# A mixture of experts in which three of eight experts get 64 slots instead of 128

## The chip, the cores and the metric

The kernel runs on one core of one Trainium2 chip. The metric is the time of one execution in microseconds of the device; the median of three runs stands for a kernel. The matrices are float32. TensorE is called PE, VectorE DVE, ScalarE ACT, GpSimd POOL and SyncE SP, as in the profile.

## The reference, cut to what matters

Two transformer blocks of two layers each are applied to 256 tokens of width 1024. The last feed-forward part is a mixture of eight experts, of which each token uses two:

```python
logits = (t @ router)                       # 256 tokens, 8 experts
top_v, top_i = lax.top_k(logits, 2)
top_w = softmax(top_v)
gate = sum(one_hot(top_i, 8) * top_w[..., None], axis=1)
y = 0
for e in range(8):                          # wg, wu: 1024 x 3584, wd: 3584 x 1024
    y = y + gate[:, e:e+1] * ((silu(t @ wg[e]) * (t @ wu[e])) @ wd[e])
```

The result of a layer norm over `ALPHA * x + y` is the output. The 512 pairs of token and expert come to 64 for an expert on average.

## The kernel before

Every product of float32 matrices is made of three fast matmuls (`mm3`): each operand is split into a high part, rounded to the fast type, and a low part, the rest; high x high, low x high and high x low are added up in PSUM. Weights come from memory in units of 1 MB on SP's queue into `raw` buffers (`Weights.load`). ACT makes the high part of a piece of 1024 columns a partition (`Weights.high`), DVE, or at times POOL, the low part (`Weights.low`), into one of five piece buffers, up to three pieces ahead of PE (`LOOK = 3`). When the low part of a unit's last piece is made, its `raw` buffer is free and SP may start the next transfer.

The order of the instructions on each engine is written out when the kernel is built. A planner (`Ctx`, `Meter`) keeps a clock for each engine with estimated costs; work beside the main chain of PE is a generator that is stepped when the clock of PE passes the moment at which its input is ready (`Ctx.tick`). In `Weights.low` the planner puts a low part on POOL if POOL's clock would end it over 1000 ns before DVE's:

```python
dve = max(m.t["vector"], m.floor) + 1.04 * n
eng = g.nc.gpsimd if g.calm or pool() + POOL < dve and not g.quiet else g.nc.vector
```

The expert stage is the end of the kernel. `begin` computes the router, and the first chunk (512 of the 3584 columns) of expert 0 for all 256 tokens. `route` finds each token's two experts, its place in the expert's list (`m.pos`), the counts and the gates. `gather` builds a 0/1 matrix (`pm`) from the places and copies the tokens of one expert with it into 128 slots, split into high and low (`xg`). `expert` goes through seven chunks of 512 columns: 16 gate products and up products (`up`, each three matmuls with a stationary 128 x 128 block of tokens and 512 moving columns of weights), Silu on ACT, the product on DVE, four transposes on PE, the split into high and low by ACT and DVE (`fT`), and eight `down` products into two banks that are kept through the expert. `finish` brings the 128 slots back to the 256 tokens with the transposed 0/1 matrix and adds them, times the gate, to the sums (`ys`). The experts go in the order 0 to 7. Eleven `raw` buffers of 1 MB feed them (two more at the start), made from memory that the other stages no longer need.

PSUM has eight banks. After the loop the largest count is read into registers; if it is over 128, a second pass over all experts handles the slots from 128 on, otherwise a branch skips it.

Of the kernel before, what the change touches and what calls it, by code (L numbers as in the profile page):

```python
# [17 lines left out]
P = 128  # L18
# [53 lines left out]
def tables3():  # L72
    j = np.arange(P)[:, None]
    t = np.arange(P)[None, :]
    up = np.where(j < t, 1.0, 0.0)
    slot = np.broadcast_to(np.arange(S)[None, :], (P, S))
    return np.ascontiguousarray(np.concatenate([up, np.ones((P, P)), slot], 1).astype(np.float32))
# [102 lines left out]
class Weights:  # L180
# [10 lines left out]
    def add(self, src, a, b, cuts):  # L191

        u = len(self.units)
        self.units.append((src, a, b))
        for i, c in enumerate(cuts):
            self.cuts.append((u, c, i == len(cuts) - 1))

    def load(self, upto=None):
        g = self.g
        m = g.m  # L200
        while self.loaded < min(upto or len(self.units), len(self.units)) and g.free["raw"]:
            src, a, b = self.units[self.loaded]
            buf = g.take("raw")
            raw = buf[:, :a * b].rearrange("p (a b) -> p a b", a=a)
            c = 0
            for s in src if isinstance(src, list) else [src]:
                n = s.shape[-1]
                g.tc.nc.sync.dma_start(raw[:, :, c:c + n], s.rearrange("(k p) n -> p k n", p=P))
                c += n
            m.t["sync"] = max(m.t["sync"], m.ready[g.key(buf)]) + 1.45 * a * b  # L210
            m.ready[g.key(buf)] = m.t["sync"] + 2000
            self.raw[self.loaded] = (buf, raw)
            self.loaded += 1

    def ahead(self, upto):
# [3 lines left out]
        while self.split <= min(upto, len(self.cuts) - 1) and g.free["piece"]:  # L219
            u, (k0, k1, c0, c1), last = self.cuts[self.split]  # L220
            if u >= self.loaded:
                self.load(u + 1)
            buf, raw = self.raw[u]
# [1692 lines left out]
E, FF = 8, 3584  # L1916
NC = FF // 512
# [10 lines left out]
def plan_expert(g, ws, li, e, begun=False):  # L1928
    a = g.a

    def up(c):
        for name in ("moe_w_gate_2", "moe_w_up_2"):
            for k0 in (0, 4):
                ws.add(a[name][li, e][k0 * P:(k0 + 4) * P, c * 512:(c + 1) * 512], 4, 512, [(0, 2, 0, 512), (2, 4, 0, 512)])

    def down(c):
        if e == E - 1 and c == NC - 1:
            for k in range(4):
                r0 = c * 512 + k * P
                ws.add(a["moe_w_down_2"][li, e][r0:r0 + P, :], 1, D, [(0, 1, 0, 512), (0, 1, 512, D)])  # L1940
            return
        for k0 in (0, 2):
            r0 = c * 512 + k0 * P
            ws.add(a["moe_w_down_2"][li, e][r0:r0 + 2 * P, :], 2, D, [(0, 1, 0, D), (1, 2, 0, D)])
# [4 lines left out]
class Moe:  # L1949


    def __init__(self, g):
# [4 lines left out]
        c3 = big[:, 4096:4608]  # L1957
        g.nc.sync.dma_start(c3, g.a["cst3"])
        self.before, self.ones, self.slot = c3[:, 0:P], c3[:, P:2 * P], c3[:, 2 * P:512]
        self.fT = [g.mid([P, 2, 4, P], F32R)]  # L1960
        self.ys = [big[:, 4608:5632], g.mid([P, D])]
# [26 lines left out]
    def last_vectors(self):  # L1988

        g = self.g  # L1990
        wb = g.big("b", [P, 2, D])
# [14 lines left out]
    def lend_slots(self):  # L2006
# [3 lines left out]
        self.slots = [g.big(s, [P, 2048]) for s in "ab"]  # L2010
# [3 lines left out]

    def after_mixer(self):
        self.lend(self.huge("b"), 3)

    def after_first(self):
# [4 lines left out]
        self.fT.append(f[:, 1024:2048].rearrange("p (a k n) -> p a k n", a=2, k=4))  # L2023


def route(g, m, po):
# [4 lines left out]
    yield lambda: len(g.free["small"]) >= 8 and g.free["t10"]  # L2031
# [7 lines left out]
    sm = [g.take("small") for _ in range(7)]  # L2039
# [3 lines left out]
    gate, pos = keep[:, 0:16], keep[:, 16:32]  # L2043
# [23 lines left out]
    m.pos, m.gate = pos, gate  # L2067
# [5 lines left out]
    m.done.mark("routed")  # L2073
    yield m.done.got("begun")

    for t in range(2):
# [9 lines left out]
        nc.vector.scalar_tensor_tensor(gate[:, e8], o1, g1, gate[:, e8], op0=ALU.mult, op1=ALU.add)  # L2086
        yield
    g.give(*sm[:6])


def begin(g, m, x, hT, ready):
# [7 lines left out]
    def at(t):  # L2099
        if t:  # L2100
# [3 lines left out]
            first.append(gather(g, m, x, 0, 0))  # L2104
# [13 lines left out]
    ft_ = m.fT[0]  # L2118
    ft = {"t": ft_, "done": False}

    def steps():
# [14 lines left out]
        ft["done"] = True  # L2136
    g.do(steps())

    def sums():
        yield lambda: ft["done"]  # L2140
# [8 lines left out]
def gather(g, m, x, e, s0):  # L2149
# [3 lines left out]

    xg_ = g.big("cab"[m.xg % 3] if not m.wb else "ca"[m.xg % 2], [P, 2, KD, P], F32R)
    m.xg += 1
    xg = [xg_[:, i] for i in range(2)]
    got = {"pm": None, "xg": xg, "n": 0}

    def steps():
        yield m.done.got("routed")  # L2160
# [4 lines left out]
        for t in range(2):  # L2165
            nc.vector.tensor_scalar(pm[:, t, :], m.slot[:, s0:s0 + P], m.pos[:, 8 * t + e:8 * t + e + 1], None,
                                    op0=ALU.is_equal)
        for q in range(2):
            yield "bank"
            p_ = g.take("bank")  # L2170
            for i in range(4):
                k = 4 * q + i
                for t in range(2):
                    nc.tensor.matmul(p_[:, i * P:(i + 1) * P], x[t][:, k * P:(k + 1) * P], pm[:, t, :],
                                     start=t == 0, stop=t == 1)
            yield
            pv = p_.rearrange("p (a b) -> p a b", a=4)
            nc.scalar.activation(xg[0][:, 4 * q:4 * q + 4], pv, AF.Copy)
            yield
            nc.vector.tensor_tensor(xg[1][:, 4 * q:4 * q + 4], pv, xg[0][:, 4 * q:4 * q + 4], op=ALU.subtract)  # L2180
            g.give(p_)
            got["n"] += 1
# [4 lines left out]
def expert(g, m, e, got, begun=None, following=None):  # L2187
# [7 lines left out]
    mine = m.count  # L2195

    def up(c):
        gu = []
        f = g.take("t20")
        for i in range(2):  # L2200
            o = g.take("bank")
            k = 0
            while k < KD:
# [3 lines left out]
                for j in range(2):  # L2207
                    mm3(g, o, xg[0][:, k, :], xg[1][:, k, :], hi[:, j, :], lo[:, j, :], k == 0, k == KD - 1)
                    k += 1
                    if j == 1:  # L2210
                        g.give(pc)
                    g.tick()
            gu.append(o)
            if i == 0:
                def sl(o=o):
                    g.act(f, o, AF.Silu)
                    g.give(o)
                g.do(sl)
        ft_ = m.fT[c % 2]
        ft = {"t": ft_, "done": False}  # L2220

        def steps():
            o = gu[1]
            nc.vector.tensor_tensor(f, o, f, op=ALU.mult)
            yield
            for i in range(4):
                nc.tensor.transpose(o[:, i * P:(i + 1) * P], f[:, i * P:(i + 1) * P], g.ident)
            g.give(f)
            yield
            pv = o.rearrange("p (a b) -> p a b", a=4)  # L2230
            nc.scalar.activation(ft_[:, 0], pv, AF.Copy)
            yield
            nc.vector.tensor_tensor(ft_[:, 1], pv, ft_[:, 0], op=ALU.subtract)
            g.give(o)
            ft["done"] = True
        g.do(steps())
        return ft

    def down(c, f):
        if not y:  # L2240
            y.extend(g.take("bank") for _ in range(2))
        g.until(lambda: f["done"])
        ft = f["t"]
        halves = e == E - 1 and c == NC - 1
        for k in range(4):
            for n in range(2):
                if n == 0 or halves:
                    hi, lo, pc = g.piece()
                s = slice(0, 512) if halves else slice(n * 512, (n + 1) * 512)
                mm3(g, y[n], ft[:, 0, k, :], ft[:, 1, k, :], hi[:, 0, s], lo[:, 0, s],  # L2250
                    c == 0 and k == 0, c == NC - 1 and k == 3)
                if n == 1 or halves:
# [17 lines left out]
    for kind, c in steps(begun):  # L2270
# [10 lines left out]
        if c == 2 and m.count == 1:  # L2281
            g.retire(*m.slots)
        if c == 3 and m.count == E - 1:
            g.do(m.last_vectors())

    def finish():
        yield m.done.got("pmT", mine)
        yield m.done.got("sums")
        yh = m.yh
# [4 lines left out]
        for t in range(2):  # L2294
            for n in range(2):
                yield "bank"
                o = g.take("bank")
                for i in range(2):
                    mm(o, m.pmT[:, tok(t)], yh[:, i, n, :], start=i == 0, stop=i == 1)
                yo = m.ys[t][:, n * 512:(n + 1) * 512]  # L2300
                gc = m.gate[:, 8 * t + e:8 * t + e + 1]
# [8 lines left out]
def experts(g, m, x, s0, got, begun=None):  # L2310
    for e in range(E):
        follow = (lambda e=e: gather(g, m, x, e + 1, s0)) if e < E - 1 else None
        got = expert(g, m, e, got, begun if e == 0 else None, follow)
# [39 lines left out]
def two_blocks(g, out):  # L2353
# [6 lines left out]
    for e in range(E):  # L2360
        plan_expert(g, g.w, 0, e, e == 0)
# [49 lines left out]
    for l in range(2):  # L2411
        mT, ready_k, over = second_mixer(g, x, l, hT, ready)
        moe = []
        after = [lambda: None, lambda: moe.append(Moe(g))][l]
# [4 lines left out]
    m, = moe  # L2419
    got, begun = begin(g, m, x, hT, ready)  # L2420
    g.early = EARLY_MOE
    experts(g, m, x, 0, got, begun)
    wb, = m.wb

    many = nc.values_load(m.cnt[0:1, 0:1], min_val=0, max_val=S)
    with g.tc.If(many > P):
        g.w = Weights(g)
        for e in range(E):
            plan_expert(g, g.w, 0, e)
        g.table = None  # L2430
        got = gather(g, m, x, 0, P)
        g.do(got["steps"])
        experts(g, m, x, P, got)
# [33 lines left out]
```

## Time and profile before

| | |
|---|---|
| median of 3 runs | 2414.9 us (2413.13 to 2416.1) |
| the profiled execution | 2413.49 us, span 2411.6 us |
| PE busy | 2357.7 us, 98% of the span |
| DVE busy | 1853.1 us, 77% |
| ACT busy | 1480.9 us, 61% |
| POOL busy | 373.6 us, 15% |
| granted clock of TensorE, mean | 0.993 |
| bytes moved | 577.70 MB, mean 240 GB/s |

The shares are averages over stages with different limits. Matmuls overlap in the record, so a busy PE may still have room; how matmuls follow one another tells more. Idle time counts on the engine that sets the pace.

### The profile page before, as it was taken

How to read it: one execution, taken by the hardware profiler on the slowest of the kernel's cores; microseconds unless marked ns; L12 is line 12 of the kernel's file. 1: busy time of each engine (PE TensorE's matmuls, PEld its weight loads, DVE VectorE, ACT ScalarE, POOL GpSimd, SP SyncE). 2: the span in 40 equal slices, each digit the busy share in tenths (PEclk: the TensorE clock that was granted, in tenths of full speed). 3: DMA queues.
4: the chain of work that ended last, by engine and by line, in shares of the span. 5: the costliest groups of instructions: out<-in, count | busy, mean ns of one | idle time of the engine just before them, and what ended most of it. 6: DMA issues, size and time to landing. Idle time of an engine off the chain costs nothing. (4 is left out here: it accounts for less than half of the span.)

```text
span 2411.6 us, 36624 instructions
## 1 busy us (share of the span) xinstructions
PE 2357.7 (98%) x13971; PEld 2039.8 (85%) x13971; DVE 1853.1 (77%) x2611; ACT 1480.9 (61%) x2126; POOL 373.6 (15%) x407
## 2 busy tenths in 40 slices
PE   8999999999999999999999899999999999999997
PEld 7799999988999988789878678888888888888785
DVE  6666987665589748765477788989898888898887
ACT  5664565465546646444446377777777777777674
POOL 4202433323043302210041300000000000000000
PEclk9999999999999999999999999999999999999998
DMA  7345555543555554455644789999999999999892
GB/s 242 123 144 189 162 190 189 179 135 128 175 175 170 190 191 155 151 158 192 209 131 141 265 310 327 349 347 346 349 359 359 332 357 350 352 346 355 316 354 93
DMA packets 317100, 577.70 MB, mean 240 GB/s; under 512 B 12818, under 2 KB 138354, under 8 KB 316660
## 3 DMA queue, kind: packets, MB, share of 16 engines
q1 hardware_dynamic: 316916, 575.28, 68.6%
q8 instruction: 111, 1.82, 0.3%
q14 instruction: 73, 0.60, 0.1%
HBM read 574.19 MB, written 1.05 MB: 239 GB/s over the span
## 5 line engine op out<-in xcount | busy, mean ns | idle before, releaser
L147 DVE TENSOR_TENSOR wlo<-raw,whi 128x1024 fp32r<-128x1024 f32 (+1 forms) x596 | 748.4, 1278 | 210.8 <-ACT whi L147 208.7
L147 ACT ACTIVATE whi<-raw 128x1024 fp32r<-128x1024 f32 (+1 forms) x628 | 637.9, 1042 | 153.1 <-PE bank L147 126.8
L147 PE MATMUL bank<-hTh,whi 128*128 128x256 f32 x1064 | 304.7, 286 | 0.2 <-ACT const L147 0.2
L147 PE MATMUL bank<-hTl,whi 128*128 128x256 f32 x1064 | 300.0, 282 | 0.0
L147 PE MATMUL bank<-hTh,wlo 128*128 128x256 f32 x1064 | 299.8, 282 | 0.0
L147 PE MATMUL bank<-whi,hTl 128*128 128x512 f32 (+2 forms) x732 | 255.3, 391 | 0.0
L147 DVE TENSOR_TENSOR wlo<-b24b,whi 128x1024 fp32r<-128x1024 f32 (+1 forms) x179 | 209.6, 1216 | 22.8 <-ACT whi L147 22.6
L147 PE MATMUL bank<-whi,b8a 128*128 128x512 f32 x672 | 212.2, 397 | 0.0
L147 PEld LDWEIGHTS bank<-hTh,whi 128*128 128x128 f32 x1064 | 200.6, 189 | 3.6 <-issue 1.5
L147 PE MATMUL bank<-whi,b8c 128*128 128x512 f32 x640 | 201.8, 396 | 0.0
L147 PEld LDWEIGHTS bank<-hTh,wlo 128*128 128x128 f32 x1064 | 200.5, 188 | 0.1
L147 PEld LDWEIGHTS bank<-hTl,whi 128*128 128x128 f32 x1064 | 200.4, 188 | 0.0
L147 POOL TENSOR_TENSOR wlo<-raw,whi 128x1024 fp32r<-128x1024 f32 (+1 forms) x32 | 81.0, 2532 | 698.7 <-ACT whi L147 695.4
L147 ACT ACTIVATE whi<-b24b 128x1024 fp32r<-128x1024 f32 (+1 forms) x180 | 179.0, 1042 | 8.3 <-PE bank L147 8.0
L147 PE MATMUL bank<-whi,b 128*128 128x512 f32 x512 | 162.9, 399 | 0.9 <-ACT b L147 0.7
L147 PEld LDWEIGHTS bank<-whi,hTl 128*128 128x128 f32 x732 | 136.7, 189 | 25.4
L147 PEld LDWEIGHTS bank<-whi,b8a 128*128 128x128 f32 x672 | 125.3, 188 | 32.0 <-issue 2.3
L147 DVE TENSOR_TENSOR wlo<-b24a,whi 128x1024 fp32r<-128x1024 f32 (+1 forms) x121 | 141.5, 1209 | 11.5 <-ACT whi L147 11.4
L147 PEld LDWEIGHTS bank<-whi,b8c 128*128 128x128 f32 x640 | 119.4, 188 | 27.6
L147 PE MATMUL bank<-whi,b8b 128*128 128x512 f32 x448 | 141.4, 396 | 0.0
L147 PE MATMUL bank<-whi,hTh 128*128 128x512 f32 (+2 forms) x348 | 139.0, 399 | 0.0
L147 PE MATMUL bank<-b8a,whi 128*128 128x256 f32 x480 | 135.4, 282 | 0.0
(306 smaller groups left out, 5292.9 us busy)
## 6 DMA issues: line engine op xcount, KB each, us to landing
raw<-in_w_in_dram SPq DMA_DIRECT2D x68, 1024.0 KB
raw<-in_w_up_dram SPq DMA_DIRECT2D x44, 1024.0 KB
raw<-in_moe_w_up_dram SPq DMA_DIRECT2D x42, 1024.0 KB
raw<-in_moe_w_gate_dram SPq DMA_DIRECT2D x41, 1024.0 KB
raw<-in_moe_w_down_dram SPq DMA_DIRECT2D x40, 1024.0 KB
b24b<-in_moe_w_up_dram SPq DMA_DIRECT2D x33, 1024.0 KB
b24b<-in_moe_w_gate_dram SPq DMA_DIRECT2D x28, 1024.0 KB
b24b<-in_moe_w_down_dram SPq DMA_DIRECT2D x27, 1024.0 KB
```

Source lines behind the costliest of these rows:

```text
L147: r = f(*a, **kw)
```

## The change

The experts are taken in an order that the chip finds from the counts. Expert 0 stays first, since its first chunk is computed before the counts are known; the other seven are ranked by their counts, and position i of the loop takes the expert of rank `RANKS[i]`. Ranks 5, 6 and 7, the three with the fewest tokens, come at positions 1, 4 and 7 and get 64 slots (`small`, `cap`). SP reads an expert's number into a register and the transfers of its weights have addresses from it (`Moe.expert`); until the numbers are known, nothing past position 0 is loaded.

In a small expert the high parts of the 64 slots stand in columns 0 to 63 of the stationary block and their low parts in columns 64 to 127 (`both`). A product is two matmuls, `both` with the high weights and `both` with the low ones, and its rows 0 to 63 and 64 to 127 have to be added. For gate that is done by a copy on ACT and a float32 product with a matrix `fold` of four unit blocks, ahead of Silu; for the block that goes to `down` the four transposes become products with `fold`; for the result of the expert the 0/1 matrix, now twice 64 columns, adds them on the way back.

The chunks are 512 or 1024 columns (`sizes`): four an expert instead of seven. A chunk of 1024 uses two banks for gate and two for up. `fT` becomes two sets of two, in a buffer (`b`) that served as a third `xg` and as an early `raw` buffer. The second pass now begins where an expert's count is over its own slots. The core of the diff:

```diff
+RANKS = [0, 5, 1, 2, 6, 3, 4, 7]
+def small(i):
+    return RANKS[i] >= 5
+def cap(i):
+    return 64 if small(i) else P
...
             src, a, b = self.units[self.loaded]
+            if callable(src):
+                src = src()
+                if src is None:
+                    break
...
-E, FF = 8, 3584
-NC = FF // 512
+NC = 4
+def sizes(begun):
+    return [512, 1024, 1024, 1024] if begun else [1024, 1024, 1024, 512]
...
+    def expert(self, i):
+        if i == 0:
+            return 0
+        if self.ids is None:
+            return None
+        if i not in self.regs:
+            self.regs[i] = self.g.tc.nc.values_load(self.ids[0:1, i:i + 1], engines=(mybir.EngineType.SP,),
+                                                    min_val=0, max_val=E - 1)
+        return self.regs[i]
...
-    nc.vector.tensor_reduce(cnt[:, 0:1], pc[:, 16:24], axis=AX.X, op=ALU.max)
-    nc.vector.tensor_copy(m.cnt, cnt[:, 0:1])
+    counts, key, rank = [cnt[:, 8 * j:8 * j + 8] for j in (1, 2, 3)]
+    nc.vector.tensor_copy(counts, pc[:, 16:24])
     g.give(po)
     m.done.mark("routed")
+    yield
...
+    def ordered(out, x):
+        nc.vector.tensor_tensor(v, at, along(x), op=ALU.mult)
+        nc.vector.tensor_reduce(out, v, axis=AX.X, op=ALU.add)
+    nc.vector.scalar_tensor_tensor(key, counts, 8.0, slot[:, 0:E], op0=ALU.mult, op1=ALU.subtract)
+    nc.vector.tensor_scalar(key[:, 0:1], key[:, 0:1], 65536.0, None, op0=ALU.add)
+    nc.vector.tensor_tensor(v, along(key), across(key), op=ALU.is_gt)
+    nc.vector.tensor_reduce(rank, v, axis=AX.X, op=ALU.add)
+    nc.vector.tensor_tensor(at, along(rank), across(m.ranks), op=ALU.is_equal)
+    ordered(key, slot[:, 0:E])
+    ids = rank.bitcast(I32)
+    nc.vector.tensor_copy(ids, key)
+    m.ids = ids
+    g.w.load()
+    yield
+    for t in range(2):
+        ordered(keep[:, 8 * t:8 * t + 8], pos[:, 8 * t:8 * t + 8])
+    m.pos = keep[:, 0:16]
+    m.done.mark("sorted")
+    ordered(key, counts)
+    nc.vector.tensor_tensor(key, key, m.spare_slots, op=ALU.add)
+    nc.vector.tensor_reduce(cnt[:, 0:1], key, axis=AX.X, op=ALU.max)
+    nc.vector.tensor_copy(m.cnt, cnt[:, 0:1])
...
-    xg_ = g.big("cab"[m.xg % 3] if not m.wb else "ca"[m.xg % 2], [P, 2, KD, P], F32R)
+    xg_ = g.big("ca"[m.xg % 2], [P, 2, KD, P], F32R)
+    split = small(i) and not again
+    n = 64 if split else P
+    xg = [xg_[:, 0, :, 64 * j:64 * j + 64] if split else xg_[:, j] for j in range(2)]
...
+    def product(o, both, h, l, rh, rl, start, stop):
+        if split:
+            mm(o, both, rh, start=start, stop=False)
+            mm(o, both, rl, start=False, stop=stop)
+        else:
+            mm3(g, o, h, l, rh, rl, start, stop)
...
+        def silu(h, o):
+            yield "t20"
+            f_ = g.take("t20")
+            if split:
+                nc.scalar.activation(f_, o, AF.Copy)
+                yield
+                mm(o, m.fold, f_, start=True, stop=True)
+                yield
+            g.act(f_, o, AF.Silu)
+            f[h] = f_
+            g.give(o)
+        def times(h, o):
+            yield lambda: h in f
+            nc.vector.tensor_tensor(f[h], o, f[h], op=ALU.mult)
+            yield
+            n = 64 if split else P
+            for j in range(4):
+                blk = f[h][:, j * P:(j + 1) * P]
+                if split:
+                    mm(o[:, j * n:(j + 1) * n], blk, m.fold[:, 0:n], start=True, stop=True)
+                else:
+                    nc.tensor.transpose(o[:, j * n:(j + 1) * n], blk, g.ident)
+            g.give(f[h])
+            yield
+            pv = o[:, 0:4 * n].rearrange("p (a b) -> p a b", a=4)
+            t = ft["t"][h]
+            hi, lo = [t[:, 0, :, 64 * s:64 * s + 64] if split else t[:, s] for s in range(2)]
+            nc.scalar.activation(hi, pv, AF.Copy)
+            yield
+            nc.vector.tensor_tensor(lo, pv, hi, op=ALU.subtract)
+            g.give(o)
+            ft["n"] += 1
```

## Rows read from the trace of the kernel before

**Rows 1.** The page's strips: the span in 40 equal slices.

```profile
PE   8999999999999999999999899999999999999997
...
GB/s 242 123 144 189 162 190 189 179 135 128 175 175 170 190 191 155 151 158 192 209 131 141 265 310 327 349 347 346 349 359 359 332 357 350 352 346 355 316 354 93
```

**Rows 2.** Window of one expert.

```profile
core 0: us, PE busy (x) PEld busy (x) DVE busy (x) ACT busy (x) POOL busy (x), PEclk, DMA share, GB/s
...
1880.70:2006.60 125.90, 125.90 (x575) 102.71 (x574) 110.51 (x110) 92.30 (x103) 0.00 (x0) 1.00 0.97 349
```

**Rows 3.** Timeline of PE: start, length, first and last of 14 products.

```profile
1699.79 0.63 PE L147 MATMUL bank<-whi,b8b 128*128 128x512 f32 x2
...
1709.59 0.63 PE L147 MATMUL bank<-whi,b8b 128*128 128x512 f32 x2
```

**Rows 4.** Waits, 1400 to 2400: who for whom, total us, times, longest.

```profile
ACT whi L147 <- PE bank L147: 30.4, 92, 0.8
```

**Rows 5.** Waits of SP's transfer queue, whole span.

```profile
SPq L208 <- DVE wlo L147: 1572.2, 448, 14.7
...
SPq L2426 <- SPq L2426: 3.4, 1, 3.4
```

**Rows 6.** Timeline of SP: the last transfer of weights.

```profile
2361.25 0.33 SPq L208 DMA_DIRECT2D b24a<-in_moe_w_down_dram  x1
```

**Rows 7.** Windows of 10 us; the last columns are DMA share and GB/s.

```profile
1380.00:1390.00 10.00, 10.00 (x61) 8.81 (x60) 4.01 (x5) 5.02 (x7) 2.36 (x1) 1.00 1.04 412
...
2370.00:2380.00 10.00, 10.00 (x45) 8.11 (x44) 8.21 (x8) 7.48 (x10) 0.00 (x0) 1.00 0.01 2
```

**Rows 8.** Timeline of DVE: three low parts and the next instruction.

```profile
1908.22 3.49 DVE L147 TENSOR_TENSOR wlo<-raw,whi 128x1024 fp32r<-128x1024 f32 x3
1911.63 0.68 DVE L147 TENSOR_TENSOR t<-bank,t 128x512 f32<-128x512 f32 x1
```

**Rows 9.** Timeline of ACT; in brackets the idle time before an instruction.

```profile
1902.50 1.06 ACT L147 ACTIVATE whi<-const 128x1024 fp32r<-128x1024 f32 x1
1903.45 1.05 ACT L147 ACTIVATE whi<-mixed 128x1024 fp32r<-128x1024 f32 x1
1905.50 0.60 ACT L147 ACTIVATE t<-bank 128x512 f32<-128x512 f32 x1 [1.01 <-PE bank L147]
```

**Rows 10.** Timeline of PE: eight gather matmuls (two records each), four transposes.

```profile
1987.33 1.95 PE L147 MATMUL bank<-t,X 128*128 128x128 f32 x16
...
2002.04 0.60 PE L147 MATMUL bank<-const,t 128*128 128x128 f32 x4
2002.39 0.71 PE L147 MATMUL bank<-whi,hTl 128*128 128x512 f32 x2
```

**Rows 11.** Lines by form, one expert: count | busy, mean ns | idle before.

```profile
L147 DVE TENSOR_TENSOR t<-bank,t 128x512 f32<-128x512 f32 x7 | 4.8, 689 | 6.4 <-PE bank L147 6.4
...
L147 ACT ACTIVATE t<-bank 128x512 f32<-128x512 f32 x7 | 4.2, 600 | 12.7 <-PE bank L147 12.7
...
L147 DVE TENSOR_TENSOR hTl<-bank,hTl 128x512 fp32r<-128x512 f32 x3 | 2.0, 683 | 0.0
...
L147 DVE CAST hTl<-bank 128x256 fp32r<-128x256 f32 x1 | 0.4, 415 | 0.0
```

**Rows 12.** Timeline of POOL at the start of an expert.

```profile
1521.43 2.41 POOL L147 TENSOR_TENSOR wlo<-b24b,whi 128x1024 fp32r<-128x1024 f32 x1 [138.84 <-ACT whi L147]
```

**Rows 13.** Timeline of DVE at the same time.

```profile
1521.27 0.68 DVE L147 TENSOR_TENSOR t<-bank,t 128x512 f32<-128x512 f32 x1
1521.87 3.05 DVE L147 TENSOR_TENSOR wlo<-b24b,whi 128x1024 fp32r<-128x1024 f32 x1
```

**Rows 14.** A window of 50 us.

```profile
1550.00:1600.00 50.00, 50.00 (x223) 40.34 (x222) 43.30 (x42) 37.06 (x41) 0.00 (x0) 1.00 1.00 366
```

**Rows 15.** Lines by form, DVE, 1356 to 1375: a small instruction of the router.

```profile
L147 DVE TENSOR_SCALAR small<-b24a,small 128x8 f32<-128x8 f32 x3 | 0.6, 227 | 0.0
```

**Rows 16.** The window around the router.

```profile
1360.00:1380.00 20.00, 19.09 (x101) 14.34 (x100) 13.46 (x31) 6.78 (x9) 5.46 (x4) 1.00 0.70 243
```

More of the change, by code (lines that the diff above doesn't have):

```diff
@@ L2022, in after_first @@
         self.pmT = f[:, 0:S]
[L2023 removed]
+        half = f[:, 1024:2048].rearrange("p (a k n) -> p a k n", a=2, k=4)
+        next(x for x in self.fT if len(x) == 1).append(half)
 def route(g, m, po):
@@ L2030, in route @@
     slot = m.slot
-    yield lambda: len(g.free["small"]) >= 8 and g.free["t10"]
+    yield lambda: len(g.free["small"]) >= 9 and len(g.free["t10"]) >= 2
     lT = g.take("t10")
@@ L2038, in route @@
     yield
-    sm = [g.take("small") for _ in range(7)]
+    sm = [g.take("small") for _ in range(8)]
+    tmp = g.take("t10")
     lg, top, ixf, sel, w2, oh = [s[:, 0:16] for s in sm[0:4]] + [sm[4][:, 0:8], sm[5]]
@@ L2195, in expert @@
     mine = m.count
-    def up(c):
[L2198 to L2201, printed above, removed]
+    split = small(i) and not again
+    size = sizes(begun)
+    def product(o, both, h, l, rh, rl, start, stop):
[4 more added lines that the diff above has]
+            mm3(g, o, h, l, rh, rl, start, stop)
+    def up(c):
+        g.until(lambda: len(m.fT) == 2)
+        nb = size[c] // 512
+        f, ft = {}, {"t": m.next_fT(), "n": 0}
+        def silu(h, o):
[25 more added lines that the diff above has]
+            hi, lo = [t[:, 0, :, 64 * s:64 * s + 64] if split else t[:, s] for s in range(2)]
+            nc.scalar.activation(hi, pv, AF.Copy)
+            yield
+            nc.vector.tensor_tensor(lo, pv, hi, op=ALU.subtract)
+            g.give(o)
+            ft["n"] += 1
+        for kind in (silu, times):
+            o = [g.take("bank") for _ in range(nb)]
             k = 0
@@ L2241, in down @@
             y.extend(g.take("bank") for _ in range(2))
[L2242 to L2245, printed above, removed]
+        blocks = size[c] // P
+        parts = i == E - 1 and c == NC - 1
+        for b in range(blocks):
+            start, stop = c == 0 and b == 0, c == NC - 1 and b == blocks - 1
+            g.until(lambda: f["n"] > b // 4)
+            ft, k = f["t"][b // 4], b % 4
             for n in range(2):
-                if n == 0 or halves:
+                if n == 0 or parts:
                     hi, lo, pc = g.piece()
[L2249 to L2252, printed above, removed]
+                s = slice(0, 512) if parts else slice(n * 512, (n + 1) * 512)
+                product(y[n], ft[:, 0, k, :], ft[:, 0, k, :], ft[:, 1, k, :], hi[:, 0, s], lo[:, 0, s], start, stop)
+                if n == 1 or parts:
                     g.give(pc)
@@ L2307, in expert, with experts @@
     return nxt
[L2310 to L2313, printed above, removed]
+def experts(g, m, x, got, begun=None, again=False):
+    for i in range(E):
+        follow = (lambda i=i: gather(g, m, x, i + 1, again)) if i < E - 1 else None
+        got = expert(g, m, i, got, begun if i == 0 else None, follow, again)
     g.drain()
```

187 lines of the change are left out of this document (100 added, 87 removed).

## The prediction

> **What bounds the kernel now.** I read the strips of the page first [rows 1]. From the 24th slice on the transfers run at 310 to 360 GB/s and PE stands at 9 tenths or more: this is the expert stage, some 40% of the span, and the change works there alone. Then the stretch of a single expert [rows 2], cut where ACT takes up the first weights of this one and of the next: an expert lasts 126 us. PE is busy in all of it, DVE for 110.5, ACT for 92.3. A busy PE proves little, since the matmuls overlap, so I looked at how they follow each other [rows 3]: 14 products of three matmuls go from 1699.79 to 1709.59, 0.700 us each, 0.2333 a matmul, with no gap. An expert has 504 of them (7 chunks of 48 up and 24 down): 117.6 us, and the transposes, the gather and the way back fill the remaining 8.4. PE sets the pace.
>
> The weights do not. An expert has 3 x 1024 x 3584 x 4 bytes = 44.04 MB, 350 GB/s at this pace. But in the expert stage ACT's high parts wait for PE's buffers, never for a landing [rows 4], and the transfer queue waits for DVE's low parts, that is for a free buffer [rows 5]. The last transfer is issued at 2361.25 [rows 6], and 2370 to 2380 shows PE full with next to nothing moving [rows 7]: the stream is some 30 us, ten buffers, ahead of its use.
>
> So the question is which engine stands behind PE. Low parts follow each other on DVE in 1.137 us (three from 1908.22 to 1911.63) [rows 8], high parts on ACT in 0.95 [rows 9]. 84 of each are 95.5 us and 79.8 us, and no edit removes one of them.
>
> **The change part by part.** *PE.* In the three small experts (positions 1, 4 and 7) a product takes two matmuls, not three. Both have all 128 stationary columns and 512 moving ones, as now, so the price stays 0.2333: 168 fewer, 39.2 us. Added are seven folds in plain float32 of 512 columns. A gather matmul of 128 such columns takes 1.95/8 = 0.244 us [rows 10], so a fold takes 0.98, 6.8 in all. The 28 transposes (0.35/4 = 0.09 us [rows 10]) become products with the fold matrix: at the gather's 0.24 at most, near half of that for half the columns; I take 0.2, 3 us more. The gather loses half its columns, about 2 us of 3.9. PE then needs 126.0 - 39.2 + 6.8 + 3 - 2 = 95 us. If PE alone decided, three times 31 = 93 us would be won.
>
> *DVE.* It does not decide alone. DVE keeps its 84 low parts. The low parts of seven chunk blocks shrink from 512 to 256 columns, 0.683 to 0.415 us [rows 11]: 1.9 us less. The gather's two become one of 512, 0.7 less. From 110.5 [rows 2] that leaves 108 us, more than PE's 95. ACT: two gather copies become one and the block copies halve, seven copies of 0.50 before the folds are new: about 92.3 + 3.5 - 2 = 94. So DVE becomes the bound of a small expert, at 108 us at least.
>
> *Waits in program order.* Today ACT idles 12.7 us and DVE 6.4 us an expert because a chunk's copy or product is queued ahead of the next high or low parts and waits for PE's last matmul of that bank [rows 11]; PE, the slower one, hides this. Behind a waiting copy stand the next high parts, behind these the low parts, and now DVE has no slack. Nothing lost gives 108; all of it, 108 + 19 = 127, no gain. The chunks of 1024 columns cut the meetings from seven to four an expert. By [rows 9] two high parts are ahead at such a point, 2.3 us of DVE's work; the copy ends some 1.3 us after PE's last piece (0.93) has its low part, the second block's copy and one high part add 1.5. That is 3.4 against 2.3, about 1.1 us at four places, so I take 5: 113 us. Each small expert saves 126 - 113 = 13 us, the three 39.
>
> *POOL.* The planner may hand a low part to POOL when its account of DVE runs 1 us past its account of POOL. It does so once an expert for a while, and there the trace shows the price: POOL's takes 2.41 us from 1521.43 [rows 12], and the low part that DVE starts at 1521.87 takes 3.05 instead of 1.22, ending 1.1 us after POOL's, while the product before it, which reads PSUM, takes its usual 0.68 [rows 13]. So one low part on POOL holds DVE's for 2.4 us and spares it 1.14. I count none more than today.
> The Trainium skill, "SBUF — State Buffer", section "Who interferes with whom", states this as a lock: a DVE instruction with two SBUF inputs and a GpSimd instruction that reads SBUF exclude each other for the whole instruction. The rows agree (1.1 us after POOL's end). By it the sum stays as it is; if the two could share, PE's 95 would bound a small expert and the time would be 2413.5 - 93 + 2 = 2322. I go by the rows.
>
> *The stream.* At 113 us a small expert draws 390 GB/s. A stretch of 10 us reaches 412 [rows 7], a 50 us one at a busy share of 1.00 holds 366 [rows 14]. At 366 the stream falls 44.04 - 41.4 = 2.7 MB behind, at 350 4.5 MB; some ten buffers ahead cover either, and a large expert after it gives at 366 2 MB back. Rows of gate and up double to 4 KB; I count nothing for it. One register load per expert on the transfer queue: the nearest is the one before the final branch, 3.4 us of that queue's wait [rows 5]. Behind it stand at most one or two transfers, hidden by the 20 us and more that data lies landed; seven of them cost 24 us if that lead is gone.
>
> *Routing.* Some 20 small DVE instructions more, about 0.2 us each by the nearest row [rows 15] (0.23): 4 us. DVE is busy 13.46 of 20 us there and PE 19.09 [rows 16], so the cost lies between nothing and 4; I take 2. Nothing of expert 1 is wanted on the queue yet.
>
> *Large experts.* Same matmuls, same lows; chunks of 1024 hold two banks for gate and two for up beside two for the result, of eight. PE stays the bound: no change; a lost bank costs at most one chain of about 2 us.
>
> Sum: 2413.5 (this execution, span 2411.6) - 39 + 2 = 2376; it lay 1.4 under the median of 2414.9, so 2377.
>
> **Rivals.** *The waits eat it.* The idle rows of [rows 11] come through nearly whole, a small expert lasts 120 to 126: 2396 to 2415. For it: DVE has no slack left. Against: ACT has 14 us.
> *Nothing is lost.* 103 to 108 us, the lower end if POOL's lows fall beside DVE's PSUM work (about 14 us an expert, at most 5 us gained): 2346 to 2361. Against: the order of the queues is written out at build time.
> *The stream is already at its limit*, 350 GB/s. Then it ends near 2365 as today, and only the lead of some 30 us shrinks to the handling of the last transfers: about 2390. Against: the waits [rows 4], the 412 GB/s [rows 7].
> *Slower:* POOL. Where the planner sees DVE late in the small experts it gives POOL lows, each 1.27 us on DVE's path. From ten an expert a small one is no shorter than a large one; at twenty it lasts 138 and the time is about 2452. Against: it did so at most once an expert here.
> *The slots do not suffice.* With more than 64 tokens in a small expert a second pass over all 352 MB adds 1000 us. Counting the reference's own router on its seed-0 inputs gives 49, 64, 68, 69, 60, 52, 100, 50; expert 0 stays first, the three smallest of the others are 50, 52 and 60. It does not happen with these.
>
> **How the numbers follow.** Small experts of 109 to 119 us: 0.56, 2359 to 2389 with a routing cost of 2 and the rounding of 1. Waits eat it: 0.18. Nothing lost: 0.12. Stream: 0.07. POOL slower: 0.06. Second pass: 0.01. About 0.2% (5 us) is what a measurement of this kernel can tell from no change, so slower begins at 2420 and faster ends at 2410: of the waits' 0.18 some 0.13 is faster, 0.05 the same. Faster 0.56 + 0.13 + 0.12 + 0.07 = 0.88, same 0.05, slower 0.07. The range 2345 to 2406 leaves out the top of the waits (0.06), POOL and the second pass (0.07) and little below.
>
> **What would show it.** Large experts still 126 us with PE full. Small ones near 113, DVE busy above 95% of them, PE's products 0.47 us long with gaps between pieces, high parts waiting for PE, not for landings. Few POOL lows, each beside a DVE low of 3 us. The last transfer some 40 us earlier than 2361 with a shorter tail behind it. Wrong if small experts come near 95 (DVE is not their bound), if ACT's highs wait for transfers, if large experts lengthen, or if PE's gaps bring its granted clock, 1.00 in all these rows, to its lower level.

## The result and the profile after

The kernel with the change takes 2377.21 us (median of 4 runs, 2374.53 to 2379.41); the kernel before took 2415.37 beside it (4 runs). The ratio is 0.9843, 95% interval 0.9826 to 0.9860. The profiled execution took 2376.09 us, span 2374.4. The forecast was 2377, in a range of 2345 to 2406.

A total that fits says little of the steps, so first the eight experts one by one, each cut where ACT takes up its first weights and where it takes up those of the next (the last one at the end of its last high part), in us:

| position | 0 | 1 | 2 | 3 | 4 | 5 | 6 | 7 |
|---|---|---|---|---|---|---|---|---|
| slots after | 128 | 64 | 128 | 128 | 64 | 128 | 128 | 64 |
| before | 173.2 | 126.2 | 126.2 | 126.1 | 125.9 | 126.1 | 125.8 | 130.2 |
| after | 178.3 | 116.6 | 125.7 | 125.8 | 111.5 | 125.7 | 125.8 | 113.4 |

The three small experts save 9.6 + 14.4 + 16.8 = 40.8 us, the large ones 1.2 together. Expert 0 loses 5.1, the stage starts 1.5 later, and what comes after the last high part is 2.0 shorter. That is the difference of the two profiled executions (2413.49 - 2376.09 = 37.4). The stages ahead are the same in both kernels; in the runs below, which share them, the first expert begins anywhere from 1327.0 to 1330.5, so the 1.5 us are spread.

The windows of the profile after, one line a stretch, to be held against the expert of before [rows 2] (the columns are the same). In order: expert 0, the small one at position 1, the large one at 2, the small one at 4, the last small one.

```profile
1330.50:1508.80 178.30, 164.00 (x767) 130.88 (x766) 148.41 (x210) 107.19 (x120) 31.78 (x17) 0.98 0.79 293
1508.80:1625.40 116.60, 106.93 (x459) 78.42 (x457) 106.91 (x100) 92.67 (x109) 24.00 (x7) 0.97 0.97 370
1625.40:1751.20 125.80, 124.97 (x566) 101.00 (x566) 113.86 (x113) 94.56 (x104) 0.00 (x0) 1.00 0.98 363
...
1877.00:1988.50 111.50, 106.66 (x458) 75.87 (x456) 106.05 (x108) 93.04 (x110) 0.00 (x0) 1.00 0.99 385
...
2240.10:2353.50 113.40, 111.18 (x442) 74.28 (x440) 107.06 (x109) 94.66 (x115) 0.00 (x0) 1.00 0.85 319
```

The reader is to see two things. In a small expert that POOL leaves alone (the fourth line) DVE is busy 106.05 of 111.50 us, 95%, where it had 110.5 of 126. And POOL does not leave all of them alone: seven instructions and 24 us of it in the first small expert, 17 and 31.8 us in expert 0. Just these two stand out: expert 0 is longer than before, and the first small one is longer than the other two. The trace has ten low parts on POOL in expert 0 (four before) and seven in the first small one (one before), and none after that.

The waits of the small expert at position 4, against [rows 4]:

```profile
PEld bank L163 <- DVE wlo L163: 19.5, 39, 1.8
ACT t L163 <- PE bank L163: 6.9, 7, 2.1
PE bank L163 <- DVE wlo L163: 4.7, 10, 1.4
DVE hTh L163 <- ACT hTh L163: 3.4, 1, 3.4
...
ACT whi L163 <- PE bank L163: 2.4, 5, 1.1
DVE wlo L163 <- ACT whi L163: 2.1, 5, 0.5
```

What is new is who waits: PE, busy without a gap in the expert of [rows 2], now stands still 4.7 us for DVE's low parts, and its weight loads, which run ahead of it, wait 19.5 us for them. The 30.4 us for which ACT's high parts waited for PE's buffers in [rows 4] are of all experts together, and that wait has not gone: from 1400 us on it is 60.0 us after. In the one expert it was 3.1 us and is 2.4. DVE itself idles 3.4 + 2.1 = 5.5 us, and the greater part of that is a single wait.

The strips of PE and of the transfers, against [rows 1], and the last transfers on SP's queue, against [rows 6]:

```profile
PE   8999999999999999989999889989999999999997
...
GB/s 246 124 127 193 167 187 186 191 136 115 177 178 162 194 215 156 107 169 187 221 156 135 200 246 333 348 378 375 366 344 364 332 389 397 371 337 360 321 373 171
```

```profile
2331.67 2.93 SPq L230 DMA_DIRECT2D raw<-in_moe_w_down_dram  x2
```

In the two slices from 1900 to 2018 us, which hold most of the small expert at position 4, the stream runs at 389 and 397 GB/s. The last transfer is issued at 2334, some 27 us earlier than before; since the end comes 37 us earlier, the stream's lead at the end is 10 us shorter. From 1400 us on ACT's high parts wait for a landing five times, at most 0.3 us each, 1.6 us in all.

### The profile page after: what moved, and what is told of

Its sections match the earlier page's. It is cut to its first block, busy times and chain, and to the rows that moved or that the text cites. A ratio compares the mean times of both kernels' runs of the same rounds, so it can differ in the third digit from the quotient of the medians.

```text
span 2374.4 us, 36554 instructions
## 1 busy us (share of the span) xinstructions
PE 2298.7 (97%) x13593; PEld 1958.9 (83%) x13593; DVE 1851.4 (78%) x2618; ACT 1490.6 (63%) x2144; POOL 407.3 (17%) x417
## 5 line engine op out<-in xcount | busy, mean ns | idle before, releaser
L163 PE MATMUL bank<-whi,b8c 128*128 128x512 f32 x752 | 247.7, 398 | 0.0
L163 PE MATMUL bank<-whi,b8a 128*128 128x512 f32 x672 | 234.2, 403 | 0.0
L163 DVE TENSOR_TENSOR wlo<-b24b,whi 128x1024 fp32r<-128x1024 f32 x168 | 201.5, 1244 | 13.5 <-ACT whi L163 12.8
L163 PE MATMUL bank<-whi,hTl 128*128 128x512 f32 (+2 forms) x540 | 196.5, 386 | 0.0
L163 PE MATMUL bank<-wlo,b8a 128*128 128x512 f32 x448 | 182.0, 406 | 8.9 <-DVE wlo L163 5.4
L163 ACT ACTIVATE whi<-b24b 128x1024 fp32r<-128x1024 f32 x172 | 174.0, 1056 | 13.9 <-PE bank L163 12.7
L163 POOL TENSOR_TENSOR wlo<-raw,whi 128x1024 fp32r<-128x1024 f32 (+1 forms) x35 | 93.5, 2672 | 515.0 <-ACT whi L163 492.3
L163 PE MATMUL bank<-wlo,b8c 128*128 128x512 f32 x432 | 173.5, 402 | 6.1 <-DVE wlo L163 6.1
L163 PEld LDWEIGHTS bank<-whi,b8c 128*128 128x128 f32 x752 | 140.9, 188 | 31.7 <-issue 1.0
L163 DVE TENSOR_TENSOR wlo<-b24a,whi 128x1024 fp32r<-128x1024 f32 x121 | 143.2, 1224 | 5.8 <-ACT whi L163 5.6
```

Of the source, the lines that this page charges most:

```text
L163: r = f(*a, **kw)
```

## The experiments

Ten kernels were run. e1 to e4 each change one thing in the kernel of after; e5 to e8 build on e1's edit, e9 and e10 on e8's. The runs of one kernel spread by 3 to 8 us, so a single run tells no smaller difference of totals; the stretches of single experts tell more. In the edits, `of_small` holds the weight units of the small experts, and "..." stands for the lines that fill it.

**e1: no low parts on POOL in the expert stage.** The first question was what the unforeseen low parts on POOL cost. In `Weights.low` the planner gives POOL nothing while `g.quiet` is above zero.

```diff
     m = g.moe
+    g.quiet += 1
     got, begun = begin(g, m, x, hT, ready)
```

> The changed kernel, with every low part from the router on left to DVE. Theory (a small expert lasts as long as DVE's own work, and a low part on POOL shuts out DVE's instructions with two SBUF inputs): the 14 low parts that POOL took between 1380 and 1600 go away, the first small expert falls from 116.6 to about 112 us like the one at position 4, PE's 3 us of idle time before the first gather go, expert 0 falls from 178 to about 174: 2377 - 8 = 2369 us, between 2365 and 2373. Rival (POOL relieves DVE, which is late): small experts and expert 0 become longer by about 1.1 us for each low part that comes back to DVE, 2377 + 10 = 2387 us or more.

Measured: 2361.44 us (5 runs, 2359.51 to 2362.08), ratio to the kernel before 0.9779 [0.9766, 0.9792], 15.8 us less than after; twice what was expected. Its windows for expert 0 and the small ones at positions 1 and 4:

```profile
1329.90:1502.20 172.30, 163.43 (x767) 130.76 (x766) 143.69 (x217) 106.97 (x120) 10.71 (x9) 0.98 0.82 303
1502.20:1611.10 108.90, 106.30 (x459) 75.95 (x457) 106.06 (x107) 93.30 (x109) 0.00 (x0) 1.00 1.01 394
1862.20:1973.70 111.50, 106.64 (x458) 75.94 (x457) 106.12 (x109) 93.03 (x110) 0.00 (x0) 1.00 0.99 385
```

Expert 0 is 6 us shorter and the first small one 7.7; the expert at position 4, which had no low part on POOL in either kernel, is the same to 0.1 us. In all 15 low parts left POOL, about 1 us of the total for each.

Where expert 0 lost its time is seen at the router's end. The timeline of after, line by line start, duration and, in brackets, idle time before:

```profile
1382.00 4.70 POOL L163 TENSOR_TENSOR wlo<-b24a,whi 128x1024 fp32r<-128x1024 f32 x2 [14.74 <-ACT whi L163]
...
1382.06 2.42 DVE L163 TENSOR_TENSOR t<-small,b24a 128x64 f32<-128x64 f32 x1
...
1384.52 2.27 DVE L163 TENSOR_TENSOR t<-t,b24a 128x64 f32<-128x64 f32 x1
...
1387.48 1.72 PE L163 MATMUL bank<-t,X 128*128 128x128 f32 x13 [2.98 <-DVE t L163]
```

and the same instructions in e1:

```profile
1382.08 0.23 DVE L163 TENSOR_TENSOR t<-small,b24a 128x64 f32<-128x64 f32 x1
...
1382.33 0.22 DVE L163 TENSOR_TENSOR t<-t,b24a 128x64 f32<-128x64 f32 x1
...
1383.26 2.05 PE L163 MATMUL bank<-t,X 128*128 128x128 f32 x16
```

Two of the new ranking instructions, 64 elements a partition and 0.22 us each, ended only with POOL's two low parts, after 2.42 and 2.27 us. Behind them on DVE stood the 0/1 matrix of expert 0's gather, and PE idled 2.98 us for it.

**e2: half of every low part in the small experts.** Is DVE what sets a small expert's time? The low parts of these experts are made for half of their columns only.

```diff
+        self.of_small = set()
...
-        eng.tensor_tensor(lo, raw, hi, op=ALU.subtract)
+        if self.cuts[i][0] in self.of_small:
+            h = lo.shape[2] // 2
+            eng.tensor_tensor(lo[:, :, 0:h], raw[:, :, 0:h], hi[:, :, 0:h], op=ALU.subtract)
+        else:
+            eng.tensor_tensor(lo, raw, hi, op=ALU.subtract)
...
```

> In the three small experts DVE makes only the first half of each low part; the second half of the piece keeps old values, so part of the computation is left out. 84 low parts of 1.14 us become 0.6 us, 45 us less of DVE in a small expert. Theory (DVE is the bound of a small expert): a small expert falls from 111 to 117 us to what PE needs, 95 to 100, or to 105 where the stream cannot follow at 420 GB/s and over; 2377 - 3 x 13 = 2338 us, between 2325 and 2350. Rival (the extra chain of copy, fold and Silu, or waits in the order of the queues, hold PE): a small expert stays within 3 us of what it was, 2368 to 2377.

Measured: 2355.84 us (one run), above the expected 2325 to 2350. The small experts took 102.2, 106.6 and 110.3 us (the first has no low part on POOL here, so against after it shows both effects). The window of the one at position 4, and its longest wait:

```profile
1863.10:1969.70 106.60, 100.74 (x462) 79.18 (x462) 69.94 (x110) 92.15 (x110) 0.00 (x0) 1.00 1.00 400
```

```profile
DVE wlo L163 <- ACT whi L163: 19.8, 49, 1.8
```

DVE's work fell by 36 us and the expert by 5. So the expert follows DVE, but not far: ACT, at 92.15 us of high parts and copies, stands close behind and now holds DVE up 49 times; PE, at 100.74, is close too; e9 and e10 go on from here.

**e3: no fold ahead of Silu.** What do the seven folds, and ACT's copy before each, cost? They are left out, so that gate stays unadded.

```diff
-            if split:
-                nc.scalar.activation(f_, o, AF.Copy)
-                yield
-                mm(o, m.fold, f_, start=True, stop=True)
-                yield
```

> In the small experts gate's two halves are not added before Silu: seven copies on ACT and seven float32 products on PE are left out, so part of the computation is missing. PE loses 6.8 us of work, ACT 3.5 to 4 in a small expert, DVE none. Theory (DVE bounds): a small expert changes by at most 2 us, 2371 to 2378. Rival (PE with its folds, or ACT's copies ahead of the high parts, bounds a small expert): 4 to 7 us less in each, 2356 to 2365.

Measured: 2367.95 us (one run), between the two expectations and 9.3 below after. At position 4 a small expert is 109.7 us, 1.8 shorter, and the last one 2.1; the first, in which POOL has low parts, 5.5. So the folds are nearly hidden behind DVE, though not quite; where POOL interferes the comparison is not clean.

**e4: the change without the 64 slots.** Order, registers, wide chunks and all else stay, but every expert has 128 slots.

```diff
-    return RANKS[i] >= 5
+    return RANKS[i] >= 8
```

> The changed kernel with its ranking, its register addresses, its chunks of 1024 columns and its buffers, but with 128 slots and three matmuls a product for every expert. Theory (the 64 slots alone bring the gain; the rest of the change costs some 5 us in expert 0): all experts from the second on last 126 us, 2414 + 5 = 2419 us, between 2414 and 2424. Rival (the wider chunks or the longer rows of the transfers bring part of the gain): below 2410.

Measured: 2420.75 us (10 runs, 2417.82 to 2423.9), ratio 1.0024 [1.0014, 1.0033]. So the 64 slots alone bring 43.5 us, and the rest of the change costs some 6 us by itself: expert 0 takes 180.9 us, 7.7 more than before. All the other experts are as before, such as those at positions 1 and 4:

```profile
1510.60:1636.60 126.00, 126.00 (x576) 103.00 (x575) 110.12 (x104) 95.01 (x103) 15.32 (x6) 1.00 0.95 354
...
1888.40:2014.30 125.90, 125.90 (x576) 103.09 (x575) 111.74 (x110) 94.97 (x103) 0.00 (x0) 1.00 0.96 351
```

The run tells two things more. POOL has low parts here too: ten in expert 0, and six (the x6 of the first line), five and three in the experts at positions 1 to 3, all of 128 slots. So it is not the small experts that bring them. And the 14 at positions 1 to 3 cost nothing: with PE as the bound these experts last 125.9 to 126.0 us.

**e5: 14 low parts of each small expert on POOL.** This is the prediction's rival on the slower side, made to happen: one low part in six goes to POOL, in e1 otherwise.

```diff
+        self.of_small = set()
...
+        if self.cuts[i][0] in self.of_small and i % 6 == 5:
+            eng = g.nc.gpsimd
...
```

> The kernel with all lows on DVE (2361.4 us, small experts 108.9, 111.4 and 113.4), but every sixth low part of a small expert, 14 of 84, put on POOL. Theory (POOL's low shuts out DVE's for its 2.4 us): each costs DVE 2.4 - 1.14 = 1.27 us, less where DVE reads PSUM meanwhile: 10 to 18 us more in each small expert, 2361 + 42 = 2403 us, between 2390 and 2415. Rival (POOL adds to DVE's capacity): DVE has 16 us less, ACT's 93 us and its waits bound a small expert at 102 to 107: 2361 - 18 = 2343 us.

Measured: 2408.09 us (one run), 46.7 above e1. The small experts took 125.5, 128.3 and 127.1 us: 16.6, 16.8 and 13.7 more for 14 low parts, so 1.0 to 1.2 us each, where 1.27 was predicted. The window of position 4, then the timelines of POOL and of DVE around one of POOL's low parts:

```profile
1877.60:2005.80 128.20, 109.84 (x457) 80.31 (x456) 108.14 (x94) 93.29 (x109) 42.44 (x14) 0.95 0.91 338
```

```profile
1908.26 2.37 POOL L163 TENSOR_TENSOR wlo<-raw,whi 128x1024 fp32r<-128x1024 f32 x1 [3.75 <-ACT whi L163]
```

```profile
1907.79 1.27 DVE L163 TENSOR_TENSOR t<-bank,t 128x512 f32<-128x512 f32 x2
1908.98 3.86 DVE L163 TENSOR_TENSOR wlo<-raw,whi 128x1024 fp32r<-128x1024 f32 x2
```

Two lows take 3.86 us instead of the 2.3 of [rows 8]. DVE has 14 low parts less than in e1 and is busy longer, 108.14 against 106.12 us: the time that it is held counts as busy. The Trainium skill, "SBUF — State Buffer", section "Who interferes with whom", says that such instructions of the two engines shut each other out; these rows agree, and those of after at the router (under e1) show it for a DVE instruction of only 64 elements a partition.

The hold is not the whole price. DVE also idles 20.1 us of the 128.2, where it idled 5.4 in e1: it waits 14.7 us for ACT's high parts, and PE waits 9.6 us for POOL's low parts themselves and 8.6 for DVE's. PE takes the pieces in order, and POOL's low parts take 3.0 us on average (42.44 / 14) against DVE's 1.2. How the 1.0 to 1.2 us divide between the hold and this wait was not measured.

**e6: numbers of the experts fixed.** Do the register loads on SP and the addresses made from them cost anything? Position i takes expert i's weights, on the base of e1, so other weights than the ranking's are used.

```diff
-        if i not in self.regs:
-            self.regs[i] = self.g.tc.nc.values_load(self.ids[0:1, i:i + 1], engines=(mybir.EngineType.SP,),
-                                                    min_val=0, max_val=E - 1)
-        return self.regs[i]
+        return i
```

> The kernel with all lows on DVE, but position i takes the weights of expert i, known when the kernel is built, whatever the ranking says, so most positions use another expert's weights. No register is loaded for the transfers and no address comes from one. Theory (the loads stand before transfers that are some 20 us ahead of their use): 2361 us, between 2358 and 2364. Rival (each register load and the longer issue hold the stream where it has no room, in the small experts): 2 to 3 us less in each expert, 2340 to 2350.

Measured: 2360.94 us (4 runs, 2359.08 to 2362.35), ratio 0.9777 [0.9762, 0.9792], the same as e1. The register loads and the addresses cost nothing that can be measured.

**e7: seven chunks of 512.** What are the wide chunks, with rows of 4 KB, worth? On the base of e1:

```diff
-NC = 4
+NC = 7
...
-    return [512, 1024, 1024, 1024] if begun else [1024, 1024, 1024, 512]
+    return [512] * 7
```

> The kernel with all lows on DVE, but seven chunks of 512 columns as in the kernel before. Gate and up come in rows of 2 KB instead of 4 KB, and gate and up end seven times an expert, not four. Theory (DVE's own work bounds a small expert, the meetings cost little): large experts 126 us, small ones 0 to 3 us longer, 2361 to 2371 us. Rival (the longer rows are needed: 44 MB in 111 us are 395 GB/s, over the 366 that the kernel before held at a full share): the lead runs out in the small experts and each lasts 116 to 120 us, 2376 to 2388 us, with high parts waiting for landings.

Measured: 2360.01 us (4 runs, 2357.22 to 2360.63), ratio 0.9771 [0.9756, 0.9786]: nothing, just below the expected range. The expert at position 4 is 0.8 us longer than in e1, the first 0.8 shorter. At position 4 the stream holds 383 GB/s with rows of 2 KB:

```profile
1859.80:1972.10 112.30, 107.56 (x457) 75.51 (x455) 108.06 (x108) 92.50 (x111) 0.00 (x0) 1.00 1.00 383
```

**e8: the result's low parts one step later.** The longest single wait of DVE in a small expert, 3.4 us, is at the result of the expert before it: in `finish` the second low part stands in DVE's queue right behind the first, ahead of weights' low parts that are ready, and waits for ACT's second copy. Here both copies come first, then the main chain goes on by one step, and the low parts follow.

```diff
         for n in range(2):
             nc.scalar.activation(yh[:, 0, n, :], y[n], AF.Copy)
+        yield
+        for n in range(2):
             nc.vector.tensor_tensor(yh[:, 1, n, :], y[n], yh[:, 0, n, :], op=ALU.subtract)
```

> The kernel with all lows on DVE, and in the way back of an expert's result DVE's two low parts are emitted only after the planner's account has ACT's two high parts done, not right behind each of them. In the small experts at positions 4 and 7 DVE stands 3.4 us behind ACT's copy there. Theory (DVE bounds a small expert, so each us that it stands still counts): 2 to 3 us less in two or three small experts, 2361 - 6 = 2355 us, between 2352 and 2359. Rival (that idle time is hidden): 2360 to 2363 us.

Measured: 2356.25 us (5 runs, 2355.1 to 2359.95), ratio 0.9761 [0.9748, 0.9775], 3.8 below e7 and 4.7 below e6, which ran on the same chip, and 21 below after. Position 4 went from 111.5 us (e1) to 109.2; the last small expert, where the same was expected, stayed (113.4 and 113.5). All that DVE waits for at position 4 is now:

```profile
DVE wlo L163 <- ACT whi L163: 2.2, 6, 0.5
DVE hTh L163 <- ACT hTh L163: 0.6, 1, 0.6
```

```profile
1860.20:1969.40 109.20, 106.83 (x458) 75.72 (x456) 106.23 (x109) 92.78 (x110) 0.00 (x0) 1.00 1.01 393
```

DVE is busy 106.23 of 109.20 us; there is little left to gain by placing.

**e9: half of the high and of the low parts,** and **e10: half of the high parts alone,** in the small experts, both on the base of e8. Together with e2 they tell which engine comes behind DVE.

> The kernel with all lows on DVE and the late result (2356 us, small experts 108.5, 109.2 and 113.5 with the end), and in small experts both ACT and DVE make only the first half of each high and low part, so part of the computation is left out. ACT then has some 52 us of work, DVE 63. Theory (DVE bounds a small expert, ACT's 93 us with its waits stand close behind, PE's 95 third): small experts fall to PE's 95 to 100 us, where 44 MB need 440 GB/s or more and the ten buffers of lead are used up, 2356 - 3 x 11 = 2323 us, between 2315 and 2335. Rival (PE itself, with its folds and products of 64 columns, needs over 105 us): 2345 us or more, with no engine waited for by PE.

> The same kernel with only ACT relieved: in small experts ACT makes half of each high part, DVE all of each low part (from partly old values, so part of the computation is left out). Theory (DVE alone bounds): small experts stay at 107 to 109 us, 2350 to 2357. Rival (ACT's high parts, each one behind copies that wait for PE, hold DVE): small experts fall to 100 to 104 us, 2330 to 2342.

Measured: e9 2340.94 us, e10 2349.36 us (one run each; the kernel before 2412.85 beside them). The windows of e9 at positions 1, 4 and 7, and of e10 at 4:

```profile
1501.30:1602.90 101.60, 99.16 (x460) 79.15 (x459) 67.74 (x110) 60.55 (x111) 0.00 (x0) 1.00 1.02 410
1852.30:1957.10 104.80, 99.82 (x459) 78.87 (x458) 68.25 (x111) 60.15 (x111) 0.00 (x0) 1.00 1.02 405
...
2206.60:2318.60 112.00, 106.08 (x443) 80.09 (x442) 67.50 (x110) 62.34 (x116) 0.00 (x0) 0.97 0.85 325
```

```profile
1857.10:1964.30 107.20, 105.09 (x459) 76.80 (x458) 106.07 (x108) 60.40 (x111) 0.00 (x0) 1.00 1.01 396
```

In e10 ACT loses 32 us of work and the expert 2: DVE, busy 106.07 of 107.20 us, is the bound alone, as expected (the total is 0.6 below the range). In e9 neither DVE (68) nor ACT (60) can be it. PE is busy for 99 to 100 us at positions 1 and 4, and waits another 2.4 and 5.0 us for low parts; the two experts take 101.6 and 104.8, not the expected 95 to 100, and the last one 112.0. There PE is busy for 106 us, at a mean granted clock of 0.97; what else keeps the last small expert at 110 us or more in every run was not looked for. The total is 6 above the range.

## Why the prediction held, step by step

*The bound moves from PE to DVE: right.* After, PE waits for low parts and DVE is busy 95% of a small expert; e10 shows DVE as bound with ACT at 60, e2 that the time falls when DVE has less to do, e4 that without the 64 slots nothing is gained. DVE's 108 us were 106. The small experts were to take 113: they took 111.5 and 113.4, and 116.6 where POOL was at work.

*5 us of waits: the size right, the place wrong.* They were put down to four gates' ends at 1.1 us. The terms given there do not make that: 1.3 and 1.5 are 2.8 and not 3.4, against 2.3 only 0.5 each, 2 us in all and 110 us for a small expert. So that 5 was met is luck. DVE's waits for high parts come to 2.1 us; 3.4 us are the one wait in `finish`, which the prediction did not have. e8 took most of it away, and position 4 fell by 2.3 us; the rest of its 3.8 to 4.7 us came in amounts of 0.8 and less from other experts and from the start, which the spread of the runs does not tell from nothing. Wide chunks were to cut the meetings from seven to four; e7, with seven, is no slower, so that reason was not a reason.

*PE's 95 us: too small by 2, the gather.* The lines by form of after, an expert's 28 products with the fold matrix (two records each) and its seven folds (two records each), at position 4, and then a gather of 64 slots, which stands in the stretch of the expert before:

```profile
L163 PE MATMUL bank<-b24a,t 128*128 128x64 f32 x56 | 7.0, 268 | 0.0
L163 PE MATMUL bank<-t,b24a 128*128 128x512 f32 x14 | 6.7, 592 | 0.0
```

```profile
L163 PE MATMUL bank<-t,X 128*128 128x64 f32 x32 | 3.7, 273 | 0.0
```

The folds take at most the 6.7 us that were costed (6.8). The busy time of a group holds a tail in which the next matmul already runs, so four products with the fold matrix are read by their start and that of the next:

```profile
1906.19 1.00 PE L163 MATMUL bank<-b24a,t 128*128 128x64 f32 x8
1907.00 0.47 PE L163 MATMUL bank<-whi,b8c 128*128 128x512 f32 x1
```

They take 0.81 us, 0.20 each, where four transposes took 0.35; with the tails it is 1.00 against 0.60 [rows 10]. Either way the 28 cost about 3 us more than the transposes, as taken. The step that failed is the gather's "half its columns, about 2 us of 3.9": it costs 3.7, so fewer columns gain next to nothing, and "near half of that for half the columns" gave the right price for the products by chance. Besides, the gather falls into the large expert ahead. That makes PE's need some 97 us. In e9 PE is busy for 99 to 100; some nine matmuls of that, 2.1 us, belong to the large expert ahead, whose last products still run on PE when ACT is at the next (the large stretch behind a small one has 566 records, for 575 before). Since DVE is the bound the missed 2 us cost nothing here; with DVE and ACT relieved (e9), PE is what comes next.

*POOL, "none more than today": wrong, and the largest miss.* 17 low parts against 7, all in expert 0 and the first small one. What the planner thought of DVE there is not in the trace. It is not the small experts that made it hand over, since e4, without them, has 24; the routing's new DVE work, just ahead of where it begins, may be the cause, but no run shows it. The price of one in a small expert was near: 1.27 us predicted, 1.0 to 1.2 in e5, about 1 in e1; in e5 it is not DVE's hold alone. Where PE is the bound the price is nothing (e4). Removing 15 of them (e1) is worth 15.8 us. The rival "POOL slower" was thus partly there, at seven low parts in one small expert instead of ten and more in each; with 14 in each (e5) a small expert is as long as a large one, as the rival had it from ten on.

*Routing, 2 us: 5.1 in its place, for another reason.* In e1, with two low parts on POOL for the four of before, expert 0 takes 172.3 us and not 173.2; at 1 us a low part, an estimate from e1's total, that leaves some 1 us for the routing itself. Beside POOL's low parts two of its 0.2-us instructions took 2.4 and 2.3 us, on the path to the first gather. With the same instructions expert 0 takes 178.3 us in after and 180.9 in e2 and e3; the mean granted clock there is 0.98 in the first and 0.96 in the others.

*The stream: right.* e9 drew 410 GB/s over 101.6 us, where the rival saw the limit at 350. High parts waited 1.6 us in all for landings in after, next to nothing. The 4-KB rows counted at nothing are worth nothing (e7), and so are the register loads (e6). Large experts stayed at 125.7. A sign that missed is the last transfer, 27 us earlier and not some 40. At the router's end the stream pauses for longer (51 and 105 GB/s in the two stretches of 10 us from 1390, where it had 86 and 358), without a high part that waits for it more than 0.3 us.

*The total.* 2377 was met in part by compensation, which is luck. Against the sum's 39 - 2 the first small expert saved 3.4 us too little, expert 0 lost 3.1 more and the stage began 1.5 later; the last small expert (16.8 for 13), the one at position 4 (14.4), the shorter end (2.0) and the large experts (1.2) made up 8.4. With POOL held off from the start, the same working would have been 16 us too high. The bounds of the main case are also 6 us too low: small experts of 109 to 119 us give 2365 to 2395 when the 2 us of routing and the 1 of rounding are added, as in the sum; 2359 to 2389 has them taken off.

*The clock, a sign of being wrong.* PE's gaps were to leave the granted clock at 1.00. In the first small expert of after its mean is 0.97, so that sign came true in part, where POOL has low parts; in e1, without them, it is 1.00.

## What to carry to other kernels

When an edit takes work from the engine that sets the pace, add up the next engine's busy time in that stretch: it, and not the work removed, gives the new time (168 matmuls less are 39 us of PE's work, and 14 us of an expert's time). Then ask what a planner, or you, will do for the engine that has become scarce: an offload to an engine that holds up the one it relieves, as POOL does DVE here, can cost more than the work handed over; on an engine with slack the same offload costs nothing (e4). And look in the waits of the new bound for the longest single one: a queue order that was free before (3.4 us in `finish`) is now paid in full.

## What was unexpected of the hardware

- A plain float32 matmul with 64 moving columns costs what one with 128 does: the gather's 16 take 3.7 us, 0.23 each, against 0.244 [rows 10]. With 512 columns one takes 0.96 (6.7 us for seven).
- A POOL low part holds up even a DVE instruction of 64 elements a partition: 0.22 us became 2.42 and 2.27.
- In stretches in which POOL's low parts make PE wait, the granted clock of TensorE has a mean of 0.97 (the first small expert of after) and 0.95 (e5, position 4), so part of the stretch ran at the lower of its two levels; PE idles 9.7 and 18.4 us there. Where it idles 2.6 to 4.8 us (e1, position 1; after, position 4) the mean is 1.00. An upper bound from these means: the lower level takes 0.03 x 116.6 = 3.5 us of the first one's 7.7 us over e1, and 0.05 x 128.2 = 6.4 of the second one's 16.8. How much of it counts, with DVE as the bound, was not separated.
- One core read 410 GB/s for 100 us (e9), and 383 with rows of 2 KB (e7).
